# Hybrid attention and RWKV layer on one core: TensorE's scores placed between the values and the turns of each attention step

## The chip, the cores and the metric

The kernel runs on one core of a Trainium2 chip. The metric is the device time of one execution in microseconds (us), lower is better. A profile is one execution, taken by the hardware profiler; its span runs from the first to the last instruction of the program.

## The reference

One decoder layer for 1024 tokens of width 1024, all in float32. Two branches read the same normalised input and are gated and added; an MLP and a gated per-layer embedding follow. The change lies in the attention branch, which has three groups of four heads (head width 64), with (window, dilation) of (128, 1), (512, 4) and (2048, 16). For each block of 128 queries and each group it computes

```python
s = jnp.einsum('bqhd,bqjhd->bqhj', qb, kg) * scale      # scores
m = jnp.max(s, axis=-1, keepdims=True)                  # maxima
e = jnp.exp(s - m)
den = jnp.sum(e, axis=-1)
o = jnp.einsum('bqhj,bqjhd->bqhd', e, vg) / den[..., None]
```

and the three groups are added, each weighted by the softmax over their logarithms of m and den. The other branch is an RWKV-7 recurrence. It is finished, but for its last stores, when the attention begins.

## The kernel before

All dense products are split into a high and a low float32r part, and each product becomes three matmuls (lines 323, 325, 327, "mm3"). The order of TensorE is written out by a planner (`Order`, line 141), which keeps its own clock `t`: each matmul that is recorded advances it by a table of costs. The planner has chains (generators such as the attention) and a list of dense work (products of the input with columns of the input weights, tiles `z`). A chain that is not due yet leaves TensorE to the next dense matmul, so dense matmuls fill every gap between two pieces of a chain. Each piece says when the next is due: for the attention this is 0.4 after the planner's estimate of the end of what the piece has set in motion on the other engines (`sch.dep + 0.4`, line 1170). During the attention, SyncE (SP), which issues all DMAs, runs in program order as well. VectorE (DVE), ScalarE (ACT) and GpSimd (POOL) are ordered by the tile framework's scheduler in this stage, not by program order alone.

The attention has 24 steps, in six units of four (a unit is a pair of heads of one group). A step takes two blocks of 128 queries of two heads, and goes through three stages that are one step apart, so that one pass of the loop (line 1154) works on three steps at once:

- `values` (line 1120) of step o: the weights times the values, matmuls `po<-PB,vkb` with 64 columns of weights, into bank s3; after every second step ScalarE copies the bank to `OTA` or `OTB`.
- `turns` (line 1106) of step t = o+1: the step's weights `SB` are transposed by TensorE (`pt<-cs,SB`), and VectorE copies them from PSUM to `PB`.
- `scores` (line 1073) of step s = t+1: q times k, matmuls `sc<-qk` over 64 rows into the banks m0 and m1; then on VectorE the mask and the maximum in one instruction for each head and block (the trace's CUSTOM_DVE_ANT_0 `SB<-sc,amask`, the order's `ISA SB,ast<-sc,amask`), and one small product `nm` for each block; then on ScalarE the exponentials `SB<-SB,nm`, which also sum the denominators.

The planner's matmul helper `mm` (line 305) and its transpose helper `tr` (line 313) know three forms: full (128 rows by 128 columns), fewer rows, and fewer columns. `z` and the turns are full, the scores use 64 rows, the values 64 columns. A width of 128 or 256 keys for each block makes a step 4 to 8 transposes and 8 to 16 value matmuls in the trace, which counts each float32 matmul of the scores and values twice.

Beside the attention a chain `sooner` (line 1818) prepares sums of MLP weights: two loads `w2e`, subtractions on VectorE (line 1827), copies on ScalarE (line 1846), stores `bs` (line 1849). When the last step is done, `combine` (line 1204) computes the weights of the three groups (`ast`), TensorE turns them (`rw`), ScalarE and VectorE make `row` of them, and TensorE spreads `row` over the heads (`cb`). Then the merge begins (`bk<-orw`), whose operands `orw` and weights `wup` are loaded into the two buffers `wr` by way of SyncE.

Of the kernel before, what the change touches and what calls it, by code (L numbers as in the profile page):

```python
# [275 lines left out]
def layer(ctx: ExitStack, tc: tile.TileContext, x, pT, wz, wup, w_out, wff1, w_ff2, w_ple, w_pleg,  # L276
# [28 lines left out]
    def mm(out_, a, b, us, start=True, stop=True):  # L305
        PE.matmul(out_, a, b, start=start, stop=stop)  # L306
        m = math.prod(a.shape[1:])
        sch.turn("full" if a.shape[0] > 64 and m > 64 else (a.shape[0], m))
        sch.t = max(sch.t, sch.written.since(a, None) - 0.1, sch.written.since(b, None) - 0.1) + us
        sch.written.put(out_, sch.t, None)  # L310
        sch.dep = sch.t
# [23 lines left out]
    def wait(cond):  # L335
        while not cond():
            yield 0.1
# [680 lines left out]
    def attention():  # L1018
# [9 lines left out]
        def stat(n=4):  # L1028
            c = col[0]
            col[0] += 8 * n  # L1030
            return st[:, c:c + 8 * n].rearrange("p (a b) -> p a b", b=n)
# [22 lines left out]
        def nat(g):  # L1054
            NAT[g] = yield from natural(g, stat)
# [11 lines left out]
        unit = lambda r: (r // 4, GORD[r // 8], r // 4 % 2)  # L1067
        blocks = lambda r: (2 * (r % 4), 2 * (r % 4) + 1)
        s = t = o = 0
# [3 lines left out]
        def scores(r):  # L1073
            n, g, hp = unit(r)
            per = T // DILS[g] // 128
            if r % 8 == 0:
                MD[g] = stat(8)
            q, k = A[n][0], A[n][1]
            sps = [psum.tile([128, 2, 256], F32, name="sc", tag=f"m{h}") for h in range(2)]
            for b in blocks(r):  # L1080
                w_ = 128 if b % max(per, 1) == 0 else 256
                k0 = (b + 1) * 128 - w_
                for h in range(2):
                    hs = slice(64 * h, 64 * h + 64)
                    mm(sps[h][:, b % 2, :w_], q[hs, b * 128:(b + 1) * 128], k[hs, k0:k0 + w_], w_ / 750)
                B[r, b] = (w_, k0)
            for b in blocks(r):
                w_, k0 = B[r, b]
                msk = amask[:, 256:384] if g == 2 else amask[:, 256 - w_:256]
                e = SB[:, b % 4]  # L1090
                mx = MD[g][:, b, 2 * hp:2 * hp + 2]
                for h in range(2):
                    V.tensor_tensor_reduce(e[:, h, :w_], sps[h][:, b % 2, :w_], msk, 1.0, -3e38, OP.add, OP.max,
                                           mx[:, h:h + 1])
                    sch.hold(f"m{h}")
                nm = small.tile([128, 2], F32, name="nm")
                V.tensor_scalar(nm, mx, -SCALE, None, op0=OP.mult)
                for h in range(2):
                    S.activation(e[:, h, :w_], e[:, h, :w_], AF.Exp, bias=nm[:, h:h + 1], scale=SCALE,
                                 accum_out=MD[g][:, b, 4 + 2 * hp + h:5 + 2 * hp + h])  # L1100
            if r % 4 == 3:
                done.add(("Q", n))
            if r % 8 == 7:
                sch.spawn(nat(g), 2, 5.0)

        def turns(r):
            for b in blocks(r):
                nk = B[r, b][0] // 128
                tp = psum.tile([128, 4, 128], F32, name="pt", tag=f"s{1 + b % 2}")
                for h in range(2):  # L1110
                    for j in range(nk):
                        tr(tp[:, 2 * h + j, :], SB[:, b % 4, h, j * 128:(j + 1) * 128], 0.107)
                P = PB[:, b % 4]
                if nk == 2:
                    V.tensor_copy(P, tp)
                else:
                    V.tensor_copy(P[:, 0::2, :], tp[:, 0::2, :])
                sch.hold(f"s{1 + b % 2}")

        def values(r, po):  # L1120
            n, g, hp = unit(r)
            d = DILS[g]
            vk, out_ = vkb[:, n % 2], OT[g][:, hp]
            for b in blocks(r):
                w_, k0 = B.pop((r, b))
                nk = w_ // 128
                for j in range(nk):
                    for h in range(2):
                        hs = slice(64 * h, 64 * h + 64)
                        mm(po[hs, b % 4, :], vk[:, k0 // 128 + j, hs], PB[:, b % 4, 2 * h + j, :], 0.16,  # L1130
                           start=j == 0, stop=j == nk - 1)
            if r % 2:
                b = 2 * (r % 4)
                src = po.rearrange("p a b -> p (a b)")
                if d == 1:
                    dst = out_[:, (b - 2) * 128:(b + 2) * 128]
                else:
                    nr = d // 2
                    r0 = (b // 4) * nr
                    dst = out_.rearrange("p (i r) -> p r i", r=d)[:, r0:r0 + nr, :]  # L1140
                    src = src.rearrange("p (r i) -> p r i", r=nr)
                S.activation(dst, src, AF.Copy)
                sch.hold("s3")
            if r % 4 == 3:
                done.add(("B", n))
                if n < 4:
                    sch.spawn(at_last(n + 2), 2)
                else:
                    load_or(5 - n, G)

        def asked(r):
            return r < 24 and len(A[r // 4].get("qk", ())) == 2 and sch.t >= max(A[r // 4]["qk"]) + LAG

        while o < 24:
            yield from wait(lambda: (asked(s) or t < s or o < t) and (o == t or ("vk", o // 4) in done))
            yield from sch.free("m0", "m1", "s1", "s2", "s3")
            sch.dep = sch.t
            at = s, t, o
            if at[2] < at[1]:
                if o % 2 == 0:  # L1160
                    po = psum.tile([128, 4, 128], F32, name="po", tag="s3")
                values(o, po)
                o += 1
            if at[1] < at[0]:
                turns(t)
                t += 1
            if asked(s):
                scores(s)
                s += 1
            yield sch.until(sch.dep + 0.4)  # L1170
        load_or(2, G)
# [93 lines left out]
    sch.spawn(inverses(), 1)  # L1265
    sch.spawn(prepare(), 1)
    sch.spawn(attention(), 1)
    for w in range(NU):
        add_rkv(w)
# [1017 lines left out]
```

## Time and profile before

| | |
|---|---|
| median of three runs | 1719.9 us (1718.79 to 1724.98) |
| profiled execution, whole | 1715.72 us |
| its span | 1713.9 us |
| TensorE busy in the span | 1695.9 us |
| VectorE, ScalarE, GpSimd busy | 1174.3, 759.4, 667.6 us |
| attention steps, first score to last value | 524.0 to 779.5 us |
| granted TensorE clock | 0.999 |

In a row of the timeline the first number is the start, the second how long the merged piece lasts with its modelled end; a bracket holds the idle time of the engine ahead of it and what ended it. Since the ends of matmuls are modelled and overlap the next start, what a matmul costs TensorE is read from start to start.

### The profile page before, as it was taken

How to read it: one execution, taken by the hardware profiler on the slowest of the kernel's cores; microseconds unless marked ns; L12 is line 12 of the kernel's file. 1: busy time of each engine (PE TensorE's matmuls, PEld its weight loads, DVE VectorE, ACT ScalarE, POOL GpSimd, SP SyncE). 2: the span in 40 equal slices, each digit the busy share in tenths (PEclk: the TensorE clock that was granted, in tenths of full speed). 3: DMA queues.
4: the chain of work that ended last, by engine and by line, in shares of the span. 5: the costliest groups of instructions: out<-in, count | busy, mean ns of one | idle time of the engine just before them, and what ended most of it. 6: DMA issues, size and time to landing. Idle time of an engine off the chain costs nothing.

```text
span 1713.9 us, 26719 instructions
## 1 busy us (share of the span) xinstructions
PE 1695.9 (99%) x10000; PEld 1386.0 (81%) x10000; DVE 1174.3 (69%) x2074; ACT 759.4 (44%) x1399; POOL 667.6 (39%) x483
## 2 busy tenths in 40 slices
PE   9999999999999999999999999999999999999998
PEld 8888888887887777776778888888888888888887
DVE  6378778677645666664765544788888888887644
ACT  5823343241425555444545465434433433443454
POOL 1222120120231323333220046877777777772211
PEclk9999999999999999999999999999999999999999
DMA  4621221221326767666543268565666566566511
GB/s 168 219 86 38 69 87 61 83 75 63 112 63 178 289 225 234 220 232 212 204 156 102 77 228 314 181 213 207 204 209 221 189 223 214 191 248 250 201 50 49
DMA packets 110916, 284.63 MB, mean 166 GB/s; under 512 B 12610, under 2 KB 12994, under 8 KB 110275
## 3 DMA queue, kind: packets, MB, share of 16 engines
q1 hardware_dynamic: 110786, 282.93, 48.2%
q8 instruction: 79, 1.29, 0.3%
q14 instruction: 51, 0.41, 0.1%
HBM read 195.45 MB, written 80.74 MB: 161 GB/s over the span
## 4 chain that ended last, share of the span: by engine, by line
PE 54%; DMA 4%; DVE 3%; ACT 2%; POOL 1%; issue 1%; SPq 0%; DVEq 0%; ACTq 0%; POOLq 0%
PE z L323 9%; PE z L325 9%; PE z L327 9%; PE bk L323 8%; PE bk L327 8%; PE bk L325 8%; DMA g<-gscr 1%; PE tp L314 1%; DMA bs<-duo 1%; POOL wl L118 1%; PE sc L306 1%; DMA bs<-OTB 1%; PE pt L314 1%; PE po L306 1%; DMA wa<-in_wff_dram 0%
## 5 line engine op out<-in xcount | busy, mean ns | idle before, releaser
L118 POOL TENSOR_TENSOR wl<-wr,wh 128x512 fp32r<-128x512 f32 (+1 forms) x112 | 157.9, 1431 | 583.0 <-ACT wh L118 556.2
L323 PE MATMUL z<-uh,wh 128*128 128x512 f32 (+1 forms) x800 | 312.6, 391 | 0.5 <-ACT uh L118 0.5
L325 PE MATMUL z<-ul,wh 128*128 128x512 f32 (+1 forms) x800 | 311.5, 389 | 1.3 <-DVE ul L118 1.3
L327 PE MATMUL z<-uh,wl 128*128 128x512 f32 (+1 forms) x800 | 312.4, 390 | 0.4 <-POOL wl L118 0.4
L118 DVE TENSOR_TENSOR tot<-tot,bk 128x512 f32<-128x512 f32 x417 | 272.9, 682 | 54.3 <-PE bk L327 54.3
L325 PEld LDWEIGHTS z<-ul,wh 128*128 128x128 f32 x800 | 150.8, 188 | 31.3 <-issue 2.8
L323 PEld LDWEIGHTS z<-uh,wh 128*128 128x128 f32 x800 | 150.7, 188 | 31.2 <-issue 4.1
L327 PEld LDWEIGHTS z<-uh,wl 128*128 128x128 f32 x800 | 150.6, 188 | 30.9 <-issue 3.4
L323 PE MATMUL bk<-duo 128*128 128x512 f32 x420 | 163.4, 389 | 0.0
L325 PE MATMUL bk<-duo 128*128 128x512 f32 x420 | 163.4, 389 | 0.0
L327 PE MATMUL bk<-duo 128*128 128x512 f32 x420 | 163.4, 389 | 0.0
L118 ACT ACTIVATE hr<-hr 128x512 f32<-128x512 f32 x96 | 60.7, 633 | 128.9 <-DVE hr L118 127.4
L118 ACT ACTIVATE wh<-wr 128x1024 fp32r<-128x1024 f32 (+2 forms) x94 | 80.8, 860 | 76.2 <-PE z L325 38.4
L118 POOL TENSOR_TENSOR duo<-sum,duo 128x512 fp32r<-128x512 f32 x60 | 83.9, 1399 | 51.4 <-ACT duo L118 51.4
L118 ACT ACTIVATE duo<-sum 128x512 fp32r<-128x512 f32 x68 | 42.7, 628 | 112.5 <-DVE sum L118 112.5
L327 PEld LDWEIGHTS bk<-duo 128*128 128x128 f32 x420 | 78.8, 188 | 16.4
L325 PEld LDWEIGHTS bk<-duo 128*128 128x128 f32 x420 | 78.8, 188 | 16.3
L323 PEld LDWEIGHTS bk<-duo 128*128 128x128 f32 x420 | 78.8, 188 | 16.3
L323 PE MATMUL z<-f,wh 128*128 128x512 f32 x212 | 82.6, 390 | 0.7 <-ACT pa L118 0.7
L327 PE MATMUL z<-f,wh 128*128 128x512 f32 x212 | 82.5, 389 | 0.0
L325 PE MATMUL z<-f,wh 128*128 128x512 f32 x212 | 82.5, 389 | 0.0
L118 DVE TENSOR_TENSOR hr<-hr,z 128x512 f32<-128x512 f32 x80 | 54.7, 684 | 34.7 <-PE z L327 32.9
(371 smaller groups left out, 3799.3 us busy)
## 6 DMA issues: line engine op xcount, KB each, us to landing
duo<-bs SPq DMA_DIRECT2D x58, 512.0 KB, 4.2
wr<-in_wz_dram SPq DMA_DIRECT2D x48, 512.0 KB, 4.5
bs<-OTB SPq DMA_DIRECT2D x35, 512.0 KB, 4.7
w2r<-in_w_ff_dram SPq DMA_DIRECT2D x32, 512.0 KB, 5.2
wr<-in_wff_dram SPq DMA_DIRECT2D x56, 256.0 KB, 3.3
w2e<-in_w_ff_dram SPq DMA_DIRECT2D x26, 512.0 KB, 6.6
hr<-p1scr SPq DMA_DIRECT2D x48, 256.0 KB, 3.1
bs<-duo SPq DMA_DIRECT2D x23, 512.0 KB, 6.0
```

Source lines behind the costliest of these rows:

```text
L118: return f(*a, **kw)
L306: PE.matmul(out_, a, b, start=start, stop=stop)
L314: PE.transpose(out_, a, ident if idn is None else idn)
L323: PE.matmul(ps, ah, bh, start=start and i == 0, stop=False, skip_group_check=not start)
L325: PE.matmul(ps, ah, bl, start=False, stop=False, skip_group_check=not start)
L327: PE.matmul(ps, al, bh, start=False, stop=i == n - 1, skip_group_check=not start)
```

## The change

`scores` is cut in two. Its matmuls stay in `scores`, which now returns the two banks; the maxima and exponentials go to a new function `weights`. In the loop the matmuls come after `values` and ahead of `turns`, and `weights` is called after `turns`. Whether a step's scores may run (`asked`) is now asked ahead of the turns.

```diff
                 B[r, b] = (w_, k0)
+            return sps
+
+        def weights(r, sps):
+            n, g, hp = unit(r)
             for b in blocks(r):
                 w_, k0 = B[r, b]
...
                 values(o, po)
                 o += 1
+            sps = scores(s) if asked(s) else None
             if at[1] < at[0]:
                 turns(t)
                 t += 1
-            if asked(s):
-                scores(s)
+            if sps:
+                weights(s, sps)
                 s += 1
             yield sch.until(sch.dep + 0.4)
```

What this does to the order of the engines is shown at three places. The first is TensorE in a pass that has all three stages (the third pass of the first unit). Before:

```order
L323 MATMUL z<-uh_126,wh 128x512
L306 MATMUL po<-PB,vkb 64x128 x4
L314 MATMUL pt<-cs,SB 128x128 x4
L306 MATMUL sc<-qk 128x128 x4
L325 MATMUL z<-ul_128,wh 128x512
```

The same engine and pass with the change:

```order
L327 MATMUL z<-uh_127,wl 128x512
L306 MATMUL po<-PB,vkb 64x128 x4
L306 MATMUL sc<-qk 128x128 x4
L314 MATMUL pt<-cs,SB 128x128 x4
L323 MATMUL z<-uh_127,wh 128x512
```

The scores have gone from behind the turns to ahead of them. Twelve passes have this form, two in each unit; in six more, the second of each unit, there are no values and the turns and scores alone change places. The number of dense matmuls between the turns and scores of one such pass and the values of the next moves too: from 13 to 18 where blocks are 128 wide, from 16 or 17 to 20 to 23 where they are wider. The last `po` and the turns of the group weights (`rw`) had 65 dense matmuls between them, and now have 35; between `rw` and the first `cb` there were 11 and now are 16. The total is unchanged, and from the second merge on TensorE's order is the same in both.

The second place is VectorE in the same pass. Before, the copies (`PB<-pt`) stand ahead of all four maxima:

```order
L118 COPY PB<-pt 128x2x128 x2
L118 ISA SB,ast<-sc,amask 128x128
L118 ISA ast 128x1
L118 ISA SB,ast<-sc,amask 128x128
L118 ISA ast 128x1
L118 ISA SB,ast<-sc,amask 128x128
L118 ISA ast 128x1
L118 TENSOR_SCALAR nm<-ast 128x2
L118 ISA SB,ast<-sc,amask 128x128
L118 ISA ast 128x1
```

With the change the scheduler puts them behind two of the four:

```order
L118 ISA SB,ast<-sc,amask 128x128
L118 ISA ast 128x1
L118 ISA SB,ast<-sc,amask 128x128
L118 ISA ast 128x1
L118 COPY PB<-pt 128x2x128 x2
L118 TENSOR_SCALAR nm<-ast 128x2
L118 ISA SB,ast<-sc,amask 128x128
L118 ISA ast 128x1
L118 ISA SB,ast<-sc,amask 128x128
L118 ISA ast 128x1
```

So the first two maxima moved ahead of the copies, and `nm`, for which the exponentials of the first block wait, now stands behind them. This is so in most passes; in the first units some keep the old order.

The third place is ScalarE ahead of the combination. Before:

```order
L118 ACTIVATE gst<-z 128x512
L118 ACTIVATE orw<-wr 128x1024
L118 ACTIVATE gst<-z 128x512
L118 ACTIVATE wh<-wr 128x768
L118 ACTIVATE row_7511<-rw 12x512 x2
```

With the change:

```order
L118 ACTIVATE gst<-z 128x512
L118 ACTIVATE orw<-wr 128x1024
L118 ACTIVATE gst<-z 128x512
L118 ACTIVATE row_7490<-rw 12x512 x2
L118 ACTIVATE wh<-wr 128x768
```

The copies of `row` moved ahead of the split of the first merge's weights (`wh<-wr`).

## The prediction

> **What bounds the kernel now.** I read the page first, then the stretch of the attention by windows, then who TensorE waits for.
>
> ```profile
> span 1713.9 us, 26719 instructions
> PE 1695.9 (99%) x10000; PEld 1386.0 (81%) x10000; DVE 1174.3 (69%) x2074; ACT 759.4 (44%) x1399; POOL 667.6 (39%) x483
> PE 54%; DMA 4%; DVE 3%; ACT 2%; POOL 1%; issue 1%; SPq 0%; DVEq 0%; ACTq 0%; POOLq 0%
> ```
>
> TensorE is busy 1695.9 of 1713.9 us, and the chain that ended last runs mostly along it. No other engine comes near. So an edit changes the time only by what it adds to or takes from TensorE's own queue: the cost of its instructions, start to start, and its waits. The next rows are the sum of eight windows of 40 us from 520 to 840 us, and two lines of the view of TensorE's waits.
>
> ```profile
> sum 320.00, PE 316.02 PEld 243.03 DVE 204.74 ACT 162.22 POOL 101.80; mean PE 39.50 PEld 30.38 DVE 25.59 ACT 20.28 POOL 12.72
> ```
>
> ```profile
> PE pt L314 <- ACT SB L118: 1.4, 4, 0.8
> PE cb L306 <- DVE row L118: 1.4, 1, 1.4
> ```
>
> In the stage that the change touches TensorE idles 320.00 - 316.02 = 4.0 us by the profile. Of these 1.4 are turns that wait for exponentials, and 1.4 the combination waiting for `row`. But ends of matmuls are modelled, so a late start right behind another instruction can hide in that instruction's length; I therefore take every cost below from start to start, out of the timeline of TensorE.
>
> **The order of forms.** This is a pass without any wait, and the end of the next, which has no scores:
>
> ```profile
> 542.08 0.39 PE L325 MATMUL z<-ul,wh 128*128 128x512 f32 x1
> 542.40 0.66 PE L306 MATMUL po<-PB,vkb 128*64 128x128 f32 x8
> 542.99 0.66 PE L314 MATMUL pt<-cs,SB 128*128 128x128 f32 x4
> 543.58 0.72 PE L306 MATMUL sc<-qk 64*128 64x128 f32 x8
> 544.22 0.50 PE L327 MATMUL z<-uh,wl 128*128 128x512 f32 x1
> 544.56 0.39 PE L323 MATMUL z<-uh,wh 128*128 128x512 f32 x1
> ...
> 547.99 0.66 PE L314 MATMUL pt<-cs,SB 128*128 128x128 f32 x4
> 548.40 0.48 PE L323 MATMUL z<-uh,wh 128*128 128x512 f32 x1
> 548.72 0.39 PE L325 MATMUL z<-ul,wh 128*128 128x512 f32 x1
> 548.95 0.39 PE L327 MATMUL z<-uh,wl 128*128 128x512 f32 x1
> ```
>
> A dense matmul behind another takes 548.95 - 548.72 = 0.23 us; ahead of the values it takes 542.40 - 542.08 = 0.32. The same four transposes take 543.58 - 542.99 = 0.59 with the scores behind them, and 548.40 - 547.99 = 0.41 with a dense matmul behind them. So a change of form is paid between neighbours, and turns beside dense matmuls, both full, pay less. [...]
>
> From the first `po` to the second dense matmul, a pass takes 544.56 - 542.40 = 2.16 us now. With the change it is values 0.59, scores, turns ahead of a dense matmul 0.41, and that dense matmul 548.72 - 548.40 = 0.32. For scores ahead of turns the nearest rows are scores ahead of other transposes (`av`), beside scores ahead of a dense matmul:
>
> ```profile
> 607.86 0.93 PE L306 MATMUL sc<-qk 64*128 64x128 f32 x8
> 608.72 1.09 PE L314 MATMUL av<-cs,v 128*128 128x128 f32 x8
> ...
> 615.25 0.93 PE L306 MATMUL sc<-qk 64*128 64x128 f32 x8
> 616.10 0.50 PE L325 MATMUL z<-ul,wh 128*128 128x512 f32 x1
> ```
>
> 0.86 and 0.85, so it does not matter which of the two follows, and I keep 544.22 - 543.58 = 0.64 for a narrow pass. The sum is 0.59 + 0.64 + 0.41 + 0.32 = 1.96, or 0.20 less. Twelve passes give **2.4 us**. Values straight ahead of scores (columns to rows) are not in the trace. I price that step like values ahead of turns. Its bounds: the change of form there could be free, or twice as dear, and 0.32 - 0.23 = 0.09 is what one costs in the rows above, so 12 x 0.09, or 1.1 us either way. In the six passes without values, I count nothing: there the scores leave a form behind on one side and gain one on the other. Nothing covers this gain or can hide it, since TensorE's queue is the bound and the dense matmuls that fill the rest of the time are the same ones.
>
> **Late turns.** Where the turns come before the exponentials are done, TensorE waits. These are the largest such places, the first in two pieces, then a wide pass, then the last turns of the last unit; with each but the first stand turns of the same size that did not wait (659.01 and 726.38):
>
> ```profile
> 535.51 0.76 PE L306 MATMUL po<-PB,vkb 128*64 128x128 f32 x8
> 537.06 0.71 PE L314 MATMUL pt<-cs,SB 128*128 128x128 f32 x2 [0.80 <-ACT SB L118]
> ...
> 538.59 0.71 PE L306 MATMUL sc<-qk 64*128 64x128 f32 x8
> ```
>
> ```profile
> 613.51 0.72 PE L314 MATMUL pt<-cs,SB 128*128 128x128 f32 x2 [0.26 <-ACT SB L118]
> 614.39 0.93 PE L314 MATMUL pt<-cs,SB 128*128 128x128 f32 x4 [0.16 <-ACT SB L118]
> ```
>
> ```profile
> 659.01 0.82 PE L314 MATMUL pt<-cs,SB 128*128 128x128 f32 x6
> 659.76 0.49 PE L306 MATMUL sc<-qk 64*128 64x128 f32 x4
> ```
>
> ```profile
> 726.38 1.09 PE L314 MATMUL pt<-cs,SB 128*128 128x128 f32 x8
> 727.23 0.48 PE L325 MATMUL z<-ul,wh 128*128 128x512 f32 x1
> ```
>
> ```profile
> 774.82 1.57 PE L314 MATMUL pt<-cs,SB 128*128 128x128 f32 x8
> 776.14 0.48 PE L325 MATMUL z<-ul,wh 128*128 128x512 f32 x1
> ```
>
> Against the pass above (0.59 and 0.59), the first loses 537.06 - 535.51 - 0.59 = 0.96 and 538.59 - 537.06 - 0.59 = 0.94. The second takes 615.25 - 613.51 = 1.74 against 659.76 - 659.01 = 0.75, or 0.99 more. The third takes 1.32 against 0.85, 0.47 more. Together 3.4 us.
>
> What happens between scores and turns shows in VectorE's and ScalarE's rows of the undisturbed pass (scores at 543.58, turned at 547.99):
>
> ```profile
> 543.47 0.75 DVE L118 COPY PB<-pt 128x256 f32<-128x256 f32 x2 [0.89 <-PE pt L314]
> 544.43 0.29 DVE L118 CUSTOM_DVE_ANT_0 SB<-sc,amask 128x128 f32<-128x128 f32 x1 [0.21 <-ACT OTA L118]
> ...
> 545.35 1.22 DVE L118 TENSOR_TENSOR qk<-qk,sw 128x1024 f32<-128x1024 f32 x1
> 546.49 0.16 DVE L118 TENSOR_SCALAR nm<-ast 128x2 f32<-128x2 f32 x1
> ...
> 546.69 0.40 ACT L118 ACTIVATE SB<-SB,nm 128x128 f32<-128x128 f32 x1 [0.53 <-DVE nm L118]
> ```
>
> The copies hide behind the scores' matmuls; foreign work of VectorE (here 1.22 us of `qk`) stands ahead of the second `nm` and makes the exponentials late. The allowance from scores to their own turns is 547.99 - 543.58 = 4.41 us. With the change it is scores 0.64, the older turns 0.41, 18 dense matmuls (0.32 + 16 x 0.23 + 0.32), values 0.59, the newer scores 0.64: 6.6 us. The chain in it gets longer by the two copies, 0.75, which now stand between the maxima. Net relief: 6.60 - 4.41 - 0.75 = 1.4 us. Of the first place (1.90 in all) 0.5 is left. The second place is the second pass of a unit, whose dense matmuls are not more than before; it gains only the scores ahead of it, 0.86, and 0.1 is left. At the last place six dense matmuls more stand ahead (1.4 us) and 0.47 is covered. So of 3.4 us I take **2.8 us**; the bounds are 0 (foreign work falls badly elsewhere) and 3.4.
>
> What is late next: VectorE's copies are needed by the values of the next pass, 18 dense matmuls later, and were needed 13 later before. The maxima start no later than before for the first two; the last two end later by the copies, inside the allowance. The banks m0 and m1 are held longer, by the turns and copies, and only chains that the planner places read them.
>
> **The end of the stage.** The copies of `row`, for which the combination waits 1.4 us, stand behind a split of weights whose load came late:
>
> ```profile
> 792.10 1.06 ACT L118 ACTIVATE orw<-wr 128x1024 fp32r<-128x1024 f32 x1 [1.77 <-DMA wr<-oscr]
> ...
> 797.44 0.84 ACT L118 ACTIVATE wh<-wr 128x768 fp32r<-128x768 f32 x1 [2.80 <-DMA wr<-in_wup_dram]
> 798.19 1.05 ACT L118 ACTIVATE row<-rw 12x512 fp32r<-12x512 f32 x2
> ```
>
> In the new order that split comes behind `row`. But the third `orw` still stands ahead of `row`, and waited 1.77 us for its load; the last `po` is now 30 dense matmuls nearer to `rw`, so the loads have less time. Bounds: 1.4 gained, or as much lost (the 1.77 come into play); nearest to the row in front, I take half the gain, **0.7 us**. DMA issues are moved within SyncE's queue but not added. On GpSimd one split changes places with its neighbour.
>
> Sum: 2.4 + 2.8 + 0.7 = 5.9 us less. The profiled execution would go from 1715.72 (span 1713.9) to 1709.8 us. It lay 4.2 us under the median of the runs shown, and the comparison is between medians, so I forecast 1719.9 - 5.9 = 1714.0 us.
>
> **The rivals.** *Only the forms.* The turns stay as late as they are, since the foreign pieces of VectorE are spread anew and ScalarE's copies for the weight sums now stand between two pairs of exponentials. For it speaks that all late turns come from such pieces, not from the pass itself. Against it, the 1.4 us of relief. Time: 1719.9 - 2.4 = 1717.5. Chance 0.18.
>
> *Everything goes.* The form into the scores is free (1.1 more), all late turns vanish (3.4), `row` is in time (1.4), and so are the other waits of the stage, 4.0 - 1.4 - 1.4 = 1.2. Gain 2.4 + 1.1 + 3.4 + 1.4 + 1.2 = 9.5: 1710.4 us. Chance 0.2.
>
> *The turns wait in every pass (slower).* In the new order the first `nm` stands on VectorE behind the copies, these wait for the older turns, and those stand on TensorE behind the new scores: a ring of copies, `nm`, exponentials and turns. [...] The ring decides once it is longer than 6.6 us. Undisturbed, it is 546.69 - 543.58 - 1.22 = 1.9 to the last pair of exponentials, two of them 0.8, and the copies 0.75: 3.5 us. So two foreign pieces of 1.22 fit and a third does not. If turns were late in the twelve passes by half of the worst one seen (1.90), that is 12 x 0.95 = 11.4, less 2.4: 1719.9 + 9.0 = 1728.9 us. Chance 0.07.
>
> *The merge is not ready.* The chain of loads for `orw` and the first merge starts nearer to the merge, and TensorE, arriving 5.2 us (2.4 + 2.8) earlier, waits there until the loads that set the pace are done. That gives back what was gained: 1719.9 us. Against it, the two waits quoted make up 2.8 of the stage's 4.0 idle us, and neither is for `orw`. Chance 0.08.
>
> **How the numbers follow.** The forecast has 0.47, with its own range of 4 us to either side. The range that is to hold the time 8 times in 10 goes from 1706 to 1726: below, everything gone plus the distance of 4.2 us between a profiled execution and the median; above, most of the way to the ring. 0.5%, about what a measurement of this kernel can tell from no change, is 8.6 us. Faster by more: most of "everything goes" (0.15) and the lower end of the forecast (0.11), 0.26. Slower: the ring, and a little for a merge that is later still, 0.08. The rest, 0.66, is within.
>
> **What would show it.** In the changed profile a pass without waits should take 1.96 us from the first `po` to the second dense matmul, with 0.59 from `po` to `sc`. TensorE's wait for ScalarE's `SB` should be well under 1.4 us, and turns of one size should take one time. `cb` should wait less than 1.4 us. The stage to the first `bk<-orw` should be shorter by about 6 us, and the distance from there to the end the same. The forecast is wrong if that distance grows (the loads), if turns wait in most passes (the ring), or if scores behind values cost 0.2 us more than they do behind turns, which takes the gain from the forms away.

## The result, and the profile after

The changed kernel takes 1709.17 us, the median of six runs (1708.4 to 1711.18). Six runs of the kernel before on the same chip have a median of 1719.35 us (1716.7 to 1724.98). The ratio is 0.9932, with an interval of 0.9914 to 0.9949: faster, by 10.2 us between these medians. The forecast was 1714.0 us, 5.9 us less than the median known then, with a range of 1706 to 1726.

The profiled executions give a smaller difference: 1715.72 before and 1708.87 after, spans 1713.9 and 1706.9, so 7.0 us. The top of the page of the kernel after, with its line of busy times and the chain that ended last by engine:

```profile
span 1706.9 us, 26712 instructions
PE 1690.3 (99%) x10000; PEld 1384.2 (81%) x10000; DVE 1184.9 (69%) x2074; ACT 758.0 (44%) x1399; POOL 665.4 (39%) x483
PE 58%; DMA 2%; DVE 1%; ACT 1%; issue 1%; POOL 0%; SPq 0%; DVEq 0%; ACTq 0%
```

TensorE is still the bound, and the chain runs along it for 58% of the span instead of 54. At the first `bk`, the end of the attention's stage, the kernel after is 6.85 us ahead in these two profiles; at the last, 7.0. So the gain is made in the stage that was changed. The sum of the eight windows of 40 us from 520 to 840 us, and two lines of the view of TensorE's waits, all of the kernel after:

```profile
sum 320.00, PE 318.15 PEld 248.47 DVE 221.32 ACT 165.37 POOL 102.19; mean PE 39.77 PEld 31.06 DVE 27.67 ACT 20.67 POOL 12.77
```

```profile
PE pt L314 <- ACT SB L118: 0.8, 1, 0.8
PE sc L306 <- DVE qk L118: 0.7, 1, 0.7
```

TensorE idles 320.00 - 318.15 = 1.85 us there instead of 4.0. By this view late turns are 0.8 us in one place instead of 1.4 in four. The combination's wait for `row`, 1.4 us, has no line any more, and scores that wait for `qk` are new. The timeline of TensorE in the third pass of the first unit shows the new order:

```profile
543.13 0.66 PE L306 MATMUL po<-PB,vkb 128*64 128x128 f32 x8
543.72 0.71 PE L306 MATMUL sc<-qk 64*128 64x128 f32 x8
544.37 0.66 PE L314 MATMUL pt<-cs,SB 128*128 128x128 f32 x4
544.78 0.47 PE L323 MATMUL z<-uh,wh 128*128 128x512 f32 x1
545.09 0.39 PE L325 MATMUL z<-ul,wh 128*128 128x512 f32 x1
```

From start to start that is values 0.59, scores 0.65, turns 0.41, the first dense matmul 0.31: 545.09 - 543.13 = 1.96 us, where it was 2.16. The two places where turns are late now, and wide turns that are not, in the same view:

```profile
537.93 1.14 PE L314 MATMUL pt<-cs,SB 128*128 128x128 f32 x4
538.83 0.48 PE L323 MATMUL z<-uh,wh 128*128 128x512 f32 x1
...
631.87 0.68 PE L314 MATMUL pt<-cs,SB 128*128 128x128 f32 x2
633.31 0.93 PE L314 MATMUL pt<-cs,SB 128*128 128x128 f32 x4 [0.76 <-ACT SB L118]
633.99 0.48 PE L325 MATMUL z<-ul,wh 128*128 128x512 f32 x1
...
657.06 0.88 PE L314 MATMUL pt<-cs,SB 128*128 128x128 f32 x6
657.69 0.48 PE L325 MATMUL z<-ul,wh 128*128 128x512 f32 x1
```

The first takes 0.90 instead of 0.41, so 0.49 is lost. The second, the last turns of the third unit, takes 633.99 - 631.87 = 2.12 instead of 0.63, so 1.49. In the kernel before the turns of that place (633.54) took 0.63 and were not late. What made them late is in VectorE's timeline of the kernel after:

```profile
626.87 1.78 DVE L1832 TENSOR_TENSOR OTB<-sum,OTB 128x512 fp32r<-128x512 f32 x1
628.57 0.28 DVE L118 CUSTOM_DVE_ANT_0 SB<-sc,amask 128x128 f32<-128x128 f32 x1
...
628.99 1.01 DVE L118 COPY PB<-pt 128x256 f32<-128x256 f32 x2
...
631.86 0.68 DVE L1832 TENSOR_TENSOR sum<-w2e,sum 128x512 f32<-128x512 f32 x1
632.46 0.15 DVE L118 TENSOR_SCALAR nm<-ast 128x2 f32<-128x2 f32 x1
```

Foreign work of another chain (`OTB`, behind a `duo` of 1.35 us) stands ahead of the first maximum, which so begins 3.7 us after its scores (624.83), and another piece stands ahead of the second `nm`. The combination, from ScalarE's and TensorE's timelines of the kernel after:

```profile
788.60 1.07 ACT L118 ACTIVATE row<-rw 12x512 fp32r<-12x512 f32 x2 [0.47 <-PE rw L314]
793.70 0.84 ACT L118 ACTIVATE wh<-wr 128x768 fp32r<-128x768 f32 x1 [4.03 <-DMA wr<-in_wup_dram]
```

```profile
792.26 0.39 PE L323 MATMUL z<-uh,wh 128*128 128x512 f32 x1
792.58 0.96 PE L306 MATMUL cb<-row,sel 64*128 64x512 f32 x3
```

In the kernel before the same two rows of TensorE were:

```profile
797.75 0.39 PE L325 MATMUL z<-ul,wh 128*128 128x512 f32 x1
799.53 1.09 PE L306 MATMUL cb<-row,sel 64*128 64x512 f32 x3 [1.39 <-DVE row L118]
```

`row` starts 0.47 us after the weights are turned. The split `wh`, whose load comes even later than before (it waits 4.03 us), stands behind it and no longer holds it up, and `cb` starts without a wait, 0.32 us behind the dense matmul ahead of it, where that was 1.78.

So the two profiles explain 7.0 us, and the medians differ by 10. The experiments ask two things: which part of the change brings the gain, and where the other 3 us are.

### The profile page after: what moved, and what is told of

It is laid out like the page before. It is cut to its first block, busy times and chain, and to the rows that moved or that the text cites. A ratio compares the mean times of both kernels' runs of the same rounds, so it can differ in the third digit from the quotient of the medians.

```text
span 1706.9 us, 26712 instructions
## 1 busy us (share of the span) xinstructions
PE 1690.3 (99%) x10000; PEld 1384.2 (81%) x10000; DVE 1184.9 (69%) x2074; ACT 758.0 (44%) x1399; POOL 665.4 (39%) x483
## 4 chain that ended last, share of the span: by engine, by line
PE 58%; DMA 2%; DVE 1%; ACT 1%; issue 1%; POOL 0%; SPq 0%; DVEq 0%; ACTq 0%
PE z L325 9%; PE z L323 9%; PE z L327 9%; PE bk L323 9%; PE bk L327 9%; PE bk L325 9%; DMA g<-gscr 1%; PE tp L314 1%; PE po L306 1%; PE sc L306 1%; PE pt L314 1%; POOL wl L118 0%; ACT wh L118 0%; DMA w2e<-in_w_ff_dram 0%; DVE g L118 0%
```

## The experiments

For each, the ratio is against runs of the kernel before on the same chip, with its interval. Behind it stands a time "at full clock". It is worked out: each execution's mean granted TensorE clock c was recorded too (to three places), I subtract (1 - c) x 1720 us, my estimate of what a lower clock costs if TensorE's work sets the time, and take the mean of the executions. In the two profiles of the result the clock is also at half in the last 2.6 us (before) and 4.2 us (after), behind TensorE's last matmul, where it costs nothing; so by these two the times are some 1 to 2 us too low (1.3 and 2.1).

**1. The kernel before, profiled again.**

> The kernel before, unchanged, profiled once more. The profiled execution shown (1715.72 us) lay 3.6 us under the median of all runs before (1719.35), while the changed kernel's profile (1708.87) lies at its median (1709.17). Theory A (late turns vary from execution to execution, since they hang on VectorE's and ScalarE's foreign work and on DMA stores): this profile is longer than 1713.9 us of span by some us, and the difference lies between the first scores and the first merge as more waits ahead of turns or values. Rival (the whole program is longer in some executions, the same everywhere): the difference is spread over the span or lies outside the attention. If the span comes out within 1 us of 1713.9, the question stays open.

This execution took 1725.27 us, 9.55 more than the one profiled first; 8.25 of that is there by the first `bk`. TensorE's longest waits in it:

```profile
PE cb L306 <- DVE row L118: 2.0, 1, 2.0
PE rc L314 <- DVE row L118: 1.8, 1, 1.8
PE pt L314 <- ACT SB L118: 1.6, 5, 0.7
PE bk L323 <- ACT wh L118: 1.6, 1, 1.6
```

The late turns are about what they were. Three other waits have grown, and behind them something stands that no wait shows. The view by windows behind the longest (the columns are the length, the busy time of PE, PEld, DVE, ACT and POOL with counts, the granted clock, the DMA share, GB/s), and TensorE's timeline from that wait on:

```profile
807.00:814.00 7.00, 7.00 (x16) 4.83 (x16) 4.61 (x7) 2.80 (x5) 2.18 (x2) 0.51 0.67 228
```

```profile
804.69 1.10 PE L306 MATMUL cb<-row,sel 64*128 64x512 f32 x3 [2.00 <-DVE row L118]
...
809.40 0.63 PE L325 MATMUL z<-ul,wh 128*128 128x512 f32 x1
809.82 0.63 PE L327 MATMUL z<-uh,wl 128*128 128x512 f32 x1
```

After the wait of 2.00 us the granted clock is 0.51 for some 7 us, and dense matmuls start 0.42 to 0.43 us apart instead of 0.23. PE counts as busy all that time. Ten such matmuls lose 10 x 0.20 = 2.0 us. Behind the wait of `rc` (592.1, clock 0.52 from 592 to 595 us) there are eight, or 1.6 us, and behind that of `bk` (865.5, clock 0.70 from 864 to 867 us) four, or 0.8: 4.4 us in all. Neither the first profile of before nor that of the kernel after has such a stretch ahead of TensorE's last matmul: in windows of 60 us the clock is 1.00 in each up to 1680 us, and from there to that matmul too.

**2. The spacing without the order.** The passes of the kernel before, as far apart as the new ones:

```diff
-            yield sch.until(sch.dep + 0.4)
+            yield sch.until(sch.dep + 1.55)
```

> Turns stay ahead of scores as before; only the next pass is due 1.15 us later by the planner's clock, so that 18 to 22 dense matmuls stand between passes, about as many as with the change (18 to 23). Theory A (the gain is 2.4 us of forms and the rest relief of late turns and of the combination): the forms' 2.2 to 2.4 us are not gained, the rest is: 4 to 6 us below before in the profile, ratio 0.995 to 0.9975, and a pass without waits costs 2.16 us from the first po to the second dense matmul. Rival B (the order alone brings it): within 1.5 us of before. Rival C (spacing alone brings it): equal to the changed kernel, 1709 us, ratio 0.993.

1720.64 us, ratio 0.9993 (0.9981 to 1.0005), at full clock 1714.1 against 1714.5 of the kernel before on this chip (0.4 less, give or take 1.3 with 95%; on all three chips together the kernel before has 1715.0). Late turns have no line left among TensorE's waits, but this one leads:

```profile
PE sc L306 <- DVE qk L118: 6.5, 3, 4.2
```

The relief of the turns is paid back by scores that come before their rotated `qk`. At the longest of these waits TensorE was ready for the scores at 697.2 us, 2.6 earlier than in the first profile of before (699.8), and `qk` was done at 701.3, 2.7 later (698.6): the chains that make it had moved too.

**3. The order without the spacing.** The kernel after, its passes as close as before:

```diff
-            yield sch.until(sch.dep + 0.4)
+            yield sch.until(sch.dep - 0.75)
```

> The changed order, but the next pass is due 1.15 us sooner by the planner's clock, so that 13 to 18 dense matmuls stand between passes, as before. Theory A: the forms are gained, 2.2 to 2.4 us, and late turns are back, at 3 to 6 us in the profile, so 0 to 3 us below before, ratio 0.998 to 1.0. Rival B (the order alone brings it): 1710 us, ratio 0.9935. Rival C (spacing alone): same as before or slower.

1718.59 us, ratio 0.9984 (0.9972 to 0.9997), at full clock 1712.5, so 2.0 less than before on this chip, give or take 1.0; the forms' 2.4 us lie within that. The waits are back:

```profile
PE bk L323 <- ACT wh L118: 1.8, 2, 1.6
PE pt L314 <- ACT SB L118: 1.6, 2, 1.1
...
PE cb L306 <- DVE OTB L118: 1.2, 1, 1.2
```

**4. The scores, with their maxima, ahead of the turns.** Here the copies stay behind the maxima, in the kernel before:

```diff
+            ask = asked(s)
+            if ask:
+                scores(s)
             if at[1] < at[0]:
...
-            if asked(s):
-                scores(s)
-                s += 1
+            s += ask
```

> The scores with their maxima and exponentials stand ahead of the turns, so that the maxima are queued ahead of the copies of the turned weights; the planner then sets 11 to 14 dense matmuls between passes. The allowance from scores to their own turns is 0.64 + 0.41 + 2.7 + 0.59 + 0.64 = 5.0 us with no copies in the chain (2.8 us undisturbed), against 6.6 with copies (3.5) in the changed kernel. Theory A: forms gained (2.3 us), slack 2.2 us instead of 3.1, so late turns between those of before and of the changed kernel: 1709 to 1714 us, ratio 0.994 to 0.997. Rival: that the maxima wait behind the copies is what costs: then faster than the changed kernel by over 1 us.

1725.22 us, ratio 1.0022 (1.0011 to 1.0033): slower, though the order of TensorE in a pass is that of the changed kernel and no turns are late. Its waits:

```profile
PE sc L306 <- DVE qk L118: 3.3, 3, 1.4
PE z L323 <- ACT wh L118: 1.6, 1, 1.6
PE cb L306 <- DVE row L118: 1.5, 1, 1.5
```

Behind 1.45 us of idle time of TensorE between 792 and 796 us the granted clock is 0.51 from 796 to 800 us and 0.64 from 800 to 804. So TensorE's order in a pass does not carry the gain by itself.

**5. The kernel after, once more.**

> The changed kernel, unchanged, profiled and timed once more beside the others of this group. Theory D (what the medians show beyond the profiles is the wait of the combination for row, 1.4 us in the profile shown and 2.0 in the second profile of the kernel before, and the half clock that came after it there: dense matmuls 0.43 us apart instead of 0.23): no wait of the combination and no stretch at 0.43 us; ratio 0.992 to 0.995 and a narrow spread of times, 2 to 4 us. Rival (the larger gain was the chance of one chip): ratio 0.996 or above, as the two first profiles had it.

1710.23 us, ratio 0.9933 (0.9915 to 0.9951), at full clock 1707.8, which is 7.7 less than before on this chip, give or take 1.5. Late turns and scores wait 0.8 and 0.7 us as in the first profile, no wait of the stage is over 0.8 us in the view of waits, and the granted clock is 0.999 as there.

The clocks of all executions settle where the other 3 us are. Of the kernel before 70 distinct executions were recorded with their clocks beside the experiments, of the kernel after 12, the six of the result among them:

| kernel | clock | executions | mean us | range us |
|---|---|---|---|---|
| before | 0.993, 0.994 | 7 | 1724.7 | 1722.9 to 1726.3 |
| before | 0.995 | 11 | 1723.4 | 1721.2 to 1726.3 |
| before | 0.996 | 19 | 1721.6 | 1719.4 to 1725.3 |
| before | 0.997 | 15 | 1721.1 | 1718.5 to 1725.6 |
| before | 0.998 | 8 | 1718.2 | 1716.4 to 1720.8 |
| before | 0.999 | 10 | 1717.4 | 1715.6 to 1719.3 |
| after | 0.998 to 1.0 | 12 | 1709.8 | 1707.9 to 1712.3 |

A line through the 70 has 1.4 us for each 0.001 of the clock. The means differ by 1721.1 - 1709.8 = 11.3 us. The mean clock is 0.9965 before and 0.9988 after: 0.0023, or 3.2 us by that line (4.0 by the formula of "at full clock"). What is left, 7.3 to 8.1 us, is near the 7.0 of the two profiles, which both have a clock of 0.999.

**6. Does the combination's wait alone bring the half clock?** The kernel before, with `cb` asked later:

```diff
-        yield None
+        yield sch.until(sch.dep + 2.5)
         for hp in range(2):
```

> The kernel before; only the first matmul of the combination (cb) is asked for 2.5 us later by the planner's clock, with 22 dense matmuls behind rw instead of 11. TensorE's order up to there is that of before. Theory D: the combination's wait is gone, and with it the half clock behind it: 1.5 us less where the clock had held, about 5 where it had not, so a ratio of 0.997 to 0.9985 and a spread of times below that of before (10 us), by some 3 us. Rival (the wait only moves, to the merge's first weights): no gain, ratio 0.999 to 1.001.

1719.83 us, ratio 0.9993 (0.9981 to 1.0006), at full clock 1714.7. The wait is gone from `cb` and stands elsewhere:

```profile
PE z L323 <- ACT oah L118: 3.4, 1, 3.4
PE rc L314 <- DVE row L118: 1.6, 1, 1.6
```

The granted clock of this execution is 0.997, so it was under the 0.999 of the first profile of before without the wait of `cb` too.

**7 and 8. More slack for three chains.** In the kernel after passes further apart (+1.0), a later due time for `qk` and for `cb`; in the kernel before the same with +1.55:

```diff
-            A[n].setdefault("qk", []).append(V.end + 0.5)
+            A[n].setdefault("qk", []).append(V.end + 2.5)
...
-            yield sch.until(sch.dep + 0.4)
+            yield sch.until(sch.dep + 1.0)
...
-        yield None
+        yield sch.until(sch.dep + 1.0)
         for hp in range(2):
```

> The changed kernel with three margins of the planner raised: a pass is due 0.6 us later (21 to 25 dense matmuls between passes), a unit's scores 2 us later after their q and k are turned, and cb 1 us later. All matmuls are the same. Theory A: the late turns left in the changed kernel (2.0 us) and its wait of scores for q and k (0.7 us) go, 1 to 2.5 us below the changed kernel. Rival (each margin moves loads and other chains, and new waits come): within 1 us of it or slower.

> The order before (turns ahead of scores) with the same margins: a pass due 1.15 us later (18 to 22 dense matmuls between passes), scores 2 us later after q and k, cb 1 us later. Against the kernel with slack and the changed order, this one differs in the order of forms alone, if both are free of waits. Theory A: 2.2 to 2.4 us slower than that one, with 2.16 against 1.96 us for a narrow pass, and 5 to 8 us faster than before. Rival B (the order of the scores itself keeps the stage in step): late turns stay, and it is less than 3 us faster than before.

On the kernel after it gives 1718.81 us, ratio 0.9987 (0.9973 to 1.0001), at full clock 1712.1: worse than without it. On the kernel before it gives 1713.6 us, ratio 0.9952 (0.9937 to 0.9967), at full clock 1710.1. The leading waits of the kernel after with slack, then of the kernel before with slack:

```profile
PE sc L306 <- DVE qk L118: 2.9, 1, 2.9
PE bk L323 <- ACT wh L118: 1.9, 2, 1.6
```

```profile
PE pt L314 <- ACT SB L118: 1.9, 4, 0.8
...
PE cb L306 <- DVE OTA L118: 0.6, 1, 0.6
```

The same edit makes long waits in the one and takes them out of the other. At full clock the kernel before with slack is 5.4 us under the kernel before on this chip, where the changed kernel is 7.7 under it. So more than half of the gain is to be had in the old order of TensorE.

**9 and 10. The copies of `row` on VectorE.** In both kernels the first copy of `row` goes from ScalarE to VectorE, and `rc` is asked 4 us later:

```diff
-        yield None
+        yield sch.until(sch.dep + 4.0)
         dst = stat(8)
...
-            S.activation(row[0:12, hs], ps, AF.Copy)
+            V.tensor_copy(row[0:12, hs], ps)
```

> The kernel before; two waits alone are taken away. The copies of row ahead of the combination run on VectorE instead of ScalarE, so they no longer stand behind the split wh of a late load; and the second turns of the group statistics (rc) are asked for 4 us later by the planner's clock, with 11 to 13 more dense matmuls ahead of them. All matmuls and the order of values, turns and scores are those of before. Theory D (in most executions of before, its rc wait of about 1.8 us, its cb wait of about 2 us and the half clock behind them make up what the medians gain beyond forms and late turns): no wait at rc and cb over 0.5 us, 4 to 7 us below before, ratio 0.996 to 0.9975. Rival (the wait moves on to the merge, as where cb alone was asked for later): ratio 0.999 to 1.001.

> The same two edits on the changed kernel, which waits at neither place. Theory D: nothing to gain, within 2 us of the changed kernel (1708 to 1712 us, ratio 0.9915 to 0.996). Rival (the edits are good for something else): over 2 us faster than the changed kernel.

The kernel before with it: 1719.91 us, ratio 0.9991 (0.9977 to 1.0005), at full clock 1714.8. The kernel after with it: 1709.51 us, ratio 0.994 (0.9921 to 0.9958). In the kernel before the waits of `rc` and `cb` are gone, and these lead:

```profile
PE z L323 <- DVE g L118: 2.3, 1, 2.3
PE sc L306 <- DVE qk L118: 2.1, 1, 2.1
```

I had thought that the waits of `rc` and `cb` alone made the kernel before slower than its first profile. That fell: without them other waits stand, and the granted clock of this execution is 0.996, where the first profile of before has 0.999.

**11 and 12. What a wait costs.** In the kernel after, eight times in the long dense stage, one small matmul waits for a copy of a freshly added tile (with `range(2)` for two more hops over ScalarE and VectorE, so a longer wait). Its result is not used, and nothing of the computation is left out.

```diff
+            if x == 3 and t == 3 and 2 <= p < 10:
+                s = small.tile([128, 2], F32, name="pw")
+                nc.vector.tensor_copy(s, tot[m][c][:, t, 0:2])
+                for _ in range(0):
+                    s2, s3 = (small.tile([128, 2], F32, name=y) for y in ("pw2", "pw"))
+                    nc.scalar.activation(s2, s, AF.Copy)
+                    nc.vector.tensor_copy(s3, s2)
+                    s = s3
+                PE.matmul(chain[t][:, 0:2], tot[m][c][:, t, 0:128], s, start=True, stop=True)
```

> The changed kernel with eight waits put into the MLP, one in every round of some 70 us: a small matmul (2 columns, result unused) that reads a sum which VectorE has just made of the matmuls ahead of it. TensorE's order is otherwise the same. Each wait should be 1.2 to 1.5 us. Theory D (short waits leave the clock alone): the cost is the sum of the waits, 10 to 12 us more than the changed kernel, dense matmuls at 0.23 us right behind them. Rival (any wait brings the half clock): 20 us or more.

> The same eight waits, each with two more hops between ScalarE and VectorE ahead of the small matmul, so about 2.5 to 3 us long. Theory D (a wait near 2 us or more is often followed by some 3 to 7 us at half clock, 1.5 to 3 us lost): the waits, 20 to 24 us, and on top 8 to 16 us of matmuls that are 0.43 us apart. Rival (the clock has nothing to do with the waits): only the 20 to 24 us.

The short waits: 1750.01 us, ratio 1.0177 (1.0149 to 1.0205). The long ones: 1747.67 us, ratio 1.0157 (1.0135 to 1.018). The waits came out longer than I had meant them to be, 1.8 us instead of 1.2 to 1.5 and 2.7 us. In the profiles of the two, short and long:

```profile
PE bk L1981 <- DVE pw L1975: 14.7, 8, 1.8
```

```profile
PE bk L1981 <- DVE pw L1979: 21.9, 8, 2.7
```

And windows around two of the short waits (1202 and 1237 us), and around a long one:

```profile
1202.00:1205.00 3.00, 1.18 (x7) 0.64 (x5) 2.87 (x6) 0.00 (x0) 2.69 (x2) 1.00 0.64 208
1205.00:1208.00 3.00, 3.00 (x14) 2.55 (x15) 0.69 (x1) 1.07 (x2) 0.00 (x0) 1.00 0.41 146
...
1237.00:1240.00 3.00, 1.31 (x6) 0.75 (x4) 2.96 (x6) 0.00 (x0) 2.86 (x2) 1.00 0.48 168
1240.00:1243.00 3.00, 2.87 (x9) 2.34 (x10) 0.76 (x2) 0.63 (x1) 0.00 (x0) 0.64 0.58 220
```

```profile
1234.00:1237.00 3.00, 2.75 (x11) 2.24 (x12) 0.86 (x2) 0.78 (x2) 0.00 (x0) 0.81 0.45 163
1237.00:1240.00 3.00, 3.00 (x10) 2.40 (x9) 0.89 (x2) 2.04 (x4) 1.92 (x2) 0.62 0.00 0
```

The two short waits are equal, 1.8 us. After the first the clock stays at 1.00; after the second it falls, to 0.64 from 1240 to 1243 us and 0.79 in the 3 us behind that (1243 to 1246). After the long one it is 0.81 and 0.62. Either stretch takes 1.7 us of clock, by length times what the clock lacks of 1: 3 x 0.36 + 3 x 0.21 and 3 x 0.19 + 3 x 0.38. How many such stretches there were is my estimate from the clocks of the two executions, 0.994 with short waits and 0.990 with long ones, where the first profile of the kernel after has 0.999: (0.999 - 0.994) x 1748.3 = 8.7 us, or five, and (0.999 - 0.990) x 1747.1 = 15.7 us, or nine, each give or take one since the clocks have three places. So by this estimate the clock fell after about five of the eight short waits and after each of the long ones, or nearly. The span with long waits (1747.1) is 40.2 us longer than the first one of the kernel after. The waits are 21.9 us of that and the clock, by this estimate, 15.7, so a wait of 2.7 us cost 5 (40.2 / 8). With the short waits the two are 14.7 and 8.7, and 23 of 41 us are explained in this way; I did not find what the rest is.

## Why the prediction was right or wrong

**The bound** held: every us gained is one of TensorE's queue, and neither the longer loads (`wh` waits 4.03 us) nor VectorE's 10.6 us more of busy time show in the time.

**The forms: right.** 1.96 us for a pass, with 0.59 from `po` to `sc`, as it was priced. The change of form from values into scores costs what the one into turns did (0.59 us from `po` to what follows it, in both). The wide passes without waits gain the same 0.20, so twelve passes are 2.4 us, and the order with the old spacing (experiment 3) is 2.0 us under the kernel before at full clock, give or take 1.0. The six passes without values, for which the prediction counted nothing, gain 0.05 each: from the last dense matmul ahead to the second one behind, 2.17 us before (from 658.78) and 2.12 after (from 655.89).

**The late turns: the relief right, its net too high.** Of the first old place 0.49 is left (0.5 forecast), and the other two are gone. The small ones that I had not counted, 0.7 us, are gone too. But 1.49 us came at the last turns of the third unit, where I counted nothing. Their exponentials come behind 3.1 us of foreign work in two pieces, and a third of 0.68: the case that the prediction described under the ring, in one pass and not in twelve. Net that is 3.4 + 0.7 - 0.49 - 1.49 = 2.1 us instead of 2.8.

**The combination: mis-sized.** I took half of the 1.4 us, against the possibility that `orw` and its load hold `row` up. They did not, and the whole wait went; from start to start it is 1.5 to 1.6 us instead of 0.7. New are 0.7 us of scores that wait for `qk`.

With these, 2.4 + 2.1 + 1.5 - 0.7 = 5.3 of the 7.0 us of the profiles are accounted for. Of the other 1.7 the six passes without values are 0.3; the rest are small differences that I did not assign. The idle time of the stage fell by 2.1 us.

**The step that failed is the last: "It lay 4.2 us under the median of the runs shown, and the comparison is between medians, so I forecast 1719.9 - 5.9".** This took the 4.2 us between the profiled execution and the median for a constant of the kernel before and after. They are not: with a clock of 0.999 the profiled execution was one of the least disturbed, since only ten of the 70 others of the kernel before have that clock. The one profiled again (clock 0.996) has longer waits on `rc`, `cb` and `bk`, and half clock behind them (4.4 us in experiment 1). The kernel after lies within 2.5 us of its profiled execution in all six of the first runs, and its twelve have a clock of 0.9988 on average. So between medians the gain of 7.0 grew by about 3. Against the profiles the sum was 1.1 us short (7.0 for 5.9); the measured median lies within the stated range, and 0.8 us below the 4 us that the forecast allowed itself.

**The rivals.** "Everything goes", with 9.5 us and 1710.4, came nearest in time and for the wrong reason: the late turns did not vanish, and some 3 of the 10.2 us are the clock. "Only the forms" is what experiment 3 shows with the old spacing. The ring and the merge that is not ready did not come.

**No single part carries the gain.** At full clock, each against the kernel before on its own chip, the order alone is worth 2.0 us, the spacing alone 0.4, both together 7.7. In most of the kernels in between long waits on `qk`, `rc`, `cb`, `oah`, `g` or `wh` came up, in changing places, since a due time that moves makes the planner place the other chains anew. That the changed kernel has none of them over 0.8 us in the stage is measured in three profiles (counting the one with `row` on VectorE); it is an outcome of its planner and not a property of the new order, as experiment 7 shows. What stays open is why one execution of the kernel before has the long waits on `rc` and `cb` and another has not. None of the variants beat the changed kernel; the one with `row` on VectorE equals it within the intervals.

## What to carry to other kernels

Count the changes of form in TensorE's queue and price them between neighbours, from start to start: that term was exact to 0.01 us per pass. Where the times of a kernel spread by 8 us, one profile is one draw: look at the granted clock of it beside that of the other executions before setting a sum against its time. And in an order that a planner makes, a moved due time moves the waits of other chains; whatever is taken from one wait must be looked for in the others.

## What was not expected of the hardware

A short wait of TensorE can cost as much again in clock, or more. In experiment 3, behind the wait of 1.2 us for `cb`, the granted clock was 0.50 from 796 to 800 us, and ten matmuls started in these 4 us; from 594 to 598 us of the same profile, at 1.00, it was twenty. So that window alone lost some 2 us. Behind the wait of 2.0 us in experiment 1 dense matmuls started 0.42 to 0.43 us apart instead of 0.23, while PE counted as busy.

The length of the wait alone does not decide. Of the two equal waits of 1.8 us in experiment 11 one left the clock at 1.00 and the other did not. In the kernel after with slack (experiment 7) the clock stayed at 1.00 from 605 to 617 us, though TensorE idled 2.86 us there between 605 and 609, ahead of `sc`.

How long a stretch lasts I estimate as twice the length of each window times what its clock lacks of 1, added up. That gives 3.4 us behind `rc` and `bk` in experiment 1, behind the second short wait of 1.8 us in experiment 11 and behind the long wait in experiment 12. It gives 6.8 or 6.9 us behind `cb` in experiments 1 and 3, from 796 us on in experiment 4, and from 805 us on in experiment 7, where the clock was 0.71, 0.50 and 0.56 in windows of 2, 3 and 3 us. So eight stretches have two lengths. What decides whether a stretch follows a wait, and which of the two it lasts, these runs do not show.
